# Keys, values and queries as a first Strassen group, the first half's indexer behind it, A11 B11 as first output product

## Chip, cores, metric

The kernel runs on one core of a Trainium2 chip. The metric is device time in microseconds, the median of 3 runs. Engines: PE (TensorE, matrix products into PSUM banks), DVE (VectorE), ACT (ScalarE), POOL (GpSimd), SP (the queue that issues nearly all DMAs). PE waits for the others through semaphores only; every engine works its own instruction list in order.

## What is computed

One layer over 1024 tokens of width 2048, all in float32:

```python
u = einsum('bsd,de->bse', h, w_in)
q, k, v, z_attn, q_idx, k_idx, w_idx, z_ssd, xbc, dt_raw = split_cols(u)
q, k, q_idx, k_idx = partial rotary of each
...
logits = relu(einsum('bqhd,bsd->bqhs', q_idx, k_idx))
score = einsum('bqhs,bqh->bqs', logits, w_idx)      # admissible keys only
_, sel = top_k(score, 256)
o_attn = softmax(q @ k[sel]) @ v[sel] * silu(z_attn)
o_ssd = rmsnorm(ssd(silu(conv(xbc)), dt) * silu(z_ssd))
sub = concat(o_attn, o_ssd) @ w_out
out = layer_norm(2 ** 0.25 * h + sub)
```

The two large products are the input projection (2048 to 6752 columns) and the output projection (2048 to 2048). Eight query heads of 128, two key/value heads, 16 indexer heads of 64, 16 SSD heads in 4 groups.

## The kernel before

**Precision and tiles.** Each float32 operand is split in a high part, rounded to the matmul's short float (ACT copies: `wh`, `xh`), and a low part, the rest (DVE or POOL subtracts: `wl`, `xl`). A product is three matmuls: high x high, high x low, low x high. The tokens are two halves of 512 (h = 0, 1; queries of half 1 may look at all keys). The projection's columns are tiles of 128: `q` 8, `k` 2, `v` 2, `z` 8 (attention gate), `qi` 8 (indexer), `misc` (indexer key, its weights, dt), `xbc` 16 and `zs` 8 (SSD and its gate).

**Stages.** The work on PE is a list of *pieces*, made in `units` (L591): a piece is one tile of 128 columns times 8 of the 16 k-blocks times 512 tokens, 24 matmuls into a PSUM bank `pj`. A plain tile is two pieces. `STAGES` (L56) lists the plain ones: (half 0: misc and the first xbc), (half 1: misc, 8 qi, the 12 k/v/q tiles, 4 xbc), (half 0: k/v, qi at half width, q). `GROUPS` (L61) then lists 14 pairs of tiles (6 of xbc, 8 of z with zs) that are computed with Strassen's scheme, in Winograd's form: with a pair of tiles, the two token halves and the two k-halves as 2x2 blocks, 7 products of 24 matmuls each instead of 8 pieces. The seven products run in four phases over all pairs (2, 2, 2, 1 products); `product` (L661) sets their weights, which are sums of blocks made by DVE from two or three loads (`t_wacc`, L871), one of them (T3) stored and loaded back; partial results P1, U2, U3 go to memory and come back (`t_save`, `t_u3`, `pre_ld`, `t_ld`), and `t_comb` (L735) adds them on DVE. The other operand is one of seven *sets* of 8 tiles each: blocks of x or their sums, which `t_xform` (L779) makes and stores once. `request` loads a set when an older one is done, `t_xst` (L762) splits it. Two sets fit.

**Output projection.** One Strassen-Winograd scheme over the whole matrix: `PRODUCTS` (L68) gives the order of the seven products. Their left operands are made from the layer's mixed outputs in memory, `mx0` and `mx1` (eight attention heads, then eight SSD blocks, per half): `t_form` (L1003) loads and adds, `t_st` splits. A11 is the attention part of half 1, A21 that of half 0, S3 = A11 - A21. The weight sums T1 to T4 are made in the background by `t_wsum` (L810) and kept in memory (`ts`).

**Background.** Indexer scores (`t_qi`, L1446, and `t_score`), the search for each query's 256th score (`t_topk`, L1511, mostly ACT passes), attention (`t_kv`, `t_attn`), the SSD scan (`t_ssd`), gates. These are generator tasks with priorities.

**What sets the order.** At build time a planner (`Flow`, with a cost model of the engines in `Sim`) emits the pieces in list order and lets tasks step in between when their priority, buffers (28 of 256 KB in pool `u`, 8 of 512 KB in `s4`) and expected times allow. Hooks start things at a piece's number: the input sums at piece 40, the output sums at 12 with priority 6. The list that results is fixed; the chip runs it with semaphores.

Of the kernel before, what the change touches and what calls it, by code (L numbers as in the profile page):

```python
# [15 lines left out]
D = 2048  # L16
# [25 lines left out]
def tile_order():  # L42
# [13 lines left out]
STAGES = [  # L56
    (0, FIRST + [("xbc", (0, 2)), ("xbc", (0, 3))], 2),
    (1, [("misc", 0)] + QI + KVQ + [("xbc", (0, j)) for j in range(4)], 3),
    (0, KVQ[:4] + QI + KVQ[4:], 3),
]  # L60
# [7 lines left out]
PRODUCTS = (("S3", "T3"), ("A11", "B11"), ("S1", "T1"), ("S2", "T2"), ("A22", "T4"), ("S4", "B22"), ("A12", "B21"))  # L68
# [501 lines left out]
class Layer:  # L570
# [20 lines left out]
    def units(self):  # L591
# [19 lines left out]

        for h, tiles, end in STAGES:
            n = len(self.sets)
            self.sets += [("x", h, 0), ("x", h, 1)]
            for part in [tiles[:3]] + [[t] for t in tiles[3:-end]] + [tiles[-end:]]:
                for u in range(2):
                    for tile in part:
                        plain(h, tile, u, n)
        for gi, pairs in enumerate(GROUPS):
# [28 lines left out]
        self.hooks.setdefault(40, []).append(self.form_tasks)  # L648
        self.hooks.setdefault(12, []).append(lambda: self.fl.add(self.t_wsum(), 6, "wsum"))
# [160 lines left out]
    def t_wsum(self):  # L810

        fl = self.fl

        def load(name, d, j):
            x = fl.new("s4", [P, 1024])
            fl.dma(x, self.w_block(name, d, j))
            return x
        for d in range(2):
            for j in range(4):
                yield Need("D", s4=4)  # L820
                x, y, z = load("B22", d, j), load("B12", d, j), fl.new("s4", [P, 1024])
                yield Need("V")
                fl.two(z, x, y, ALU.subtract)
                yield Need("")
                fl.dma(self.tsum["T3", d, j], z)
                fl.free(z)
                yield Need("D", s4=1)
# [3 lines left out]
                fl.free(z)  # L831
                yield Need("V")
# [1448 lines left out]
```

## Time and profile before

| | |
|---|---|
| median of 3 runs | 1735.62 us (1734.35 to 1738.17) |
| profiled run | 1736.13 us, of which its span 1734.3 us |
| granted TensorE clock, mean | 0.986 |
| ACT busy | 993.8 us (57%) |
| POOL busy | 176.7 us (10%) |
| memory read / written | 306.32 / 97.65 MB |

A profile names engines by busy time; matmuls overlap, so PE's busy share says when PE had work, and the spacing of matmul starts says what one costs. Windows give, for a stretch of time, each engine's busy time and count, the granted clock, the DMA engines' share and the rate. In a timeline row, brackets hold the idle time before an instruction and what ended it. All operations go through a helper, so one line (L313) stands for all; groups are told apart by names of buffers.

### The profile page before, as it was taken

To read this page: it belongs to the slowest core of one execution; us is meant where nothing else is said; L and a number is where in the kernel's file an instruction comes from. 1 tells how busy PE (TensorE), PEld (TensorE's weight loads), DVE (VectorE), ACT (ScalarE), POOL (GpSimd) and SP (SyncE) were. 2 spreads that over 40 slices of the span, in tenths; PEclk is the share of its full clock that TensorE was granted. 3 is DMA by queue.
4 is the path that set the end of the run, shared out by engine and by line. 5 is a ranking of instruction groups with operands and counts; after the bars stand their busy time and mean duration, and the time that the engine had idled before them with its cause. 6 is when DMAs were issued, how large, how long until landed. Compare 5 with 4: busy or idle time off the path is not lost. (4 is left out here: it accounts for less than half of the span.)

```text
span 1734.3 us, 24108 instructions
## 1 busy us (share of the span) xinstructions
PE 1667.1 (96%) x8188; PEld 1380.5 (80%) x8188; DVE 1293.0 (75%) x2309; ACT 993.8 (57%) x1753; POOL 176.7 (10%) x194
## 2 busy tenths in 40 slices
PE   9999999999999999999999999999999979999987
PEld 7877888787887778888888888777888768888865
DVE  5778866747577778785887678877678757549998
ACT  5755554797797777854555556745775454432320
POOL 0000000000000000121022310302130000000110
PEclk9999999999989999999999999999999989999989
DMA  8543225887643686567863598789979979967654
GB/s 321 191 154 101 84 99 182 280 278 279 208 157 108 205 304 228 195 227 274 309 203 123 182 351 300 252 258 346 314 225 330 327 236 348 343 227 273 213 168 150
DMA packets 185156, 405.58 MB, mean 234 GB/s; under 512 B 19144, under 2 KB 59208, under 8 KB 185032
## 3 DMA queue, kind: packets, MB, share of 16 engines
q1 hardware_dynamic: 184600, 403.65, 68.5%
q8 instruction: 64, 1.05, 0.2%
q14 instruction: 60, 0.49, 0.1%
q10 hardware_dynamic: 432, 0.39, 0.1%
HBM read 306.32 MB, written 97.65 MB: 233 GB/s over the span
## 5 line engine op out<-in xcount | busy, mean ns | idle before, releaser
L313 PE MATMUL pj<-xh,wh 128*128 128x512 f32 (+1 forms) x1264 | 495.9, 392 | 3.4 <-ACT u L313 3.4
L313 PE MATMUL pj<-xh,wl 128*128 128x512 f32 (+1 forms) x1264 | 486.0, 385 | 5.6 <-DVE wl L313 5.6
L313 PE MATMUL pj<-xl,wh 128*128 128x512 f32 (+1 forms) x1264 | 484.9, 384 | 0.0
L313 DVE TENSOR_TENSOR wl<-wr,wh 128x1024 fp32r<-128x1024 f32 (+1 forms) x189 | 230.5, 1220 | 179.8 <-ACT wh L313 176.7
L313 PEld LDWEIGHTS pj<-xh,wl 128*128 128x128 f32 x1264 | 238.3, 189 | 56.1 <-DVE wl L313 8.2
L313 PEld LDWEIGHTS pj<-xh,wh 128*128 128x128 f32 x1264 | 238.7, 189 | 48.3 <-ACT u L313 4.3
L313 PEld LDWEIGHTS pj<-xl,wh 128*128 128x128 f32 x1264 | 238.7, 189 | 42.2 <-DVE xl L313 0.4
L313 ACT ACTIVATE wh<-wr 128x1024 fp32r<-128x1024 f32 (+2 forms) x192 | 198.4, 1034 | 113.8 <-PE pj L313 74.7
L313 PE MATMUL pj<-xh,s 128*128 128x512 f32 (+1 forms) x640 | 204.5, 385 | 2.7 <-ACT wh L313 2.6
L313 PE MATMUL a<-u,u 128*128 128x512 f32 (+3 forms) x766 | 175.8, 352 | 11.2 <-DVE u L313 7.9
L313 PEld LDWEIGHTS a<-u,u 128*128 128x128 f32 x766 | 126.9, 191 | 44.8 <-DVE u L313 12.5
L313 PEld LDWEIGHTS pj<-xh,s 128*128 128x128 f32 x640 | 119.8, 191 | 25.3 <-ACT wh L313 2.8
L313 ACT ACTIVATE u<-u 128x512 f32<-128x512 f32 (+4 forms) x169 | 94.5, 565 | 77.8 <-DVE u L313 64.1
L313 ACT ACTIVATE u<-s,sm 128x768 bf16<-128x768 int16 (+7 forms) x132 | 129.7, 983 | 15.5 <-DVE sm L313 13.5
L313 PE MATMUL pj<-xl,s 128*128 128x512 f32 (+1 forms) x320 | 121.8, 381 | 0.8 <-DVE xl L313 0.8
L313 DVE TENSOR_TENSOR u<-u,u 128x512 f32<-128x512 f32 (+7 forms) x187 | 107.6, 587 | 14.4 <-DMA u<-o 8.3
L313 ACT ACTIVATE a<-a 128x512 f32<-128x512 f32 (+3 forms) x160 | 75.5, 503 | 73.9 <-PE a L313 70.3
L313 ACT ACTIVATE u<-a 128x512 fp32r<-128x512 f32 (+4 forms) x117 | 53.5, 474 | 109.2 <-DVE u L313 56.2
L313 DVE TENSOR_TENSOR wr<-wr,wr 128x1024 f32<-128x1024 f32 (+1 forms) x69 | 88.4, 1283 | 15.3 <-DMA wr<-wt 14.4
L313 ACT ACTIVATE u<-pj 128x512 f32<-128x512 f32 (+1 forms) x83 | 46.1, 561 | 87.7 <-PE pj L313 87.6
L313 PE MATMUL pj<-wh,xh 128*128 128x512 f32 x208 | 84.2, 405 | 8.8 <-DVE xh L313 7.2
L313 DVE TENSOR_TENSOR s<-wr,s 128x1024 fp32r<-128x1024 f32 (+2 forms) x55 | 67.1, 1221 | 31.8 <-ACT s L313 31.8
(262 smaller groups left out, 2633.8 us busy)
## 6 DMA issues: line engine op xcount, KB each, us to landing
wr<-wt SPq DMA_DIRECT2D x222, 512.0 KB, 4.6
s<-wo SPq DMA_DIRECT2D x35, 512.0 KB, 5.4
u<-u SPq DMA_DIRECT2D x70, 256.0 KB, 5.0
ts<-s SPq DMA_DIRECT2D x32, 512.0 KB, 5.6
wr<-ts SPq DMA_DIRECT2D x32, 512.0 KB, 5.4
s<-xt SPq DMA_DIRECT2D x25, 512.0 KB, 9.2
u<-mx SPq DMA_DIRECT2D x42, 256.0 KB, 5.4
wr<-wo SPq DMA_DIRECT2D x20, 512.0 KB
```

The costliest lines, as they stand in the source:

```text
L313: f(*args, **kw)
```

## The change

`STAGES` and `GROUPS` become one `PLAN`. Stage two loses the k/v/q tiles; after it stands a first Strassen group of six pairs (k0 k1, v0 v1, q_n q_(n+4)); then the first half's indexer tiles; then the old group with z and zs exchanged within their pairs. The first output product is A11 B11, S3 T3 the second. The input sums start at piece 12. The output sums are made in halves of 512 columns in buffers of `u`, with two hooks and priority 5. Attention keeps fewer buffers, and both head groups of half 0 wait for half 1's second only.

```diff
+PLAN = [
     (0, FIRST + [("xbc", (0, 2)), ("xbc", (0, 3))], 2),
-    (1, [("misc", 0)] + QI + KVQ + [("xbc", (0, j)) for j in range(4)], 3),
-    (0, KVQ[:4] + QI + KVQ[4:], 3),
-]
-GROUPS = [
-    [(("xbc", (1, j)), ("xbc", (3, j))) for j in range(4)] + [(("xbc", (2, j)), ("xbc", (2, 2 + j))) for j in range(2)]
-    + [(("z", n), ("zs", (n // 2, n % 2))) for n in range(8)],
+    (1, [("misc", 0)] + QI + [("xbc", (0, j)) for j in range(4)], 3),
+    [(("k", 0), ("k", 1)), (("v", 0), ("v", 1))] + [(("q", n), ("q", n + 4)) for n in range(4)],
+    (0, QI, 3),
+    [(("xbc", (1, j)), ("xbc", (3, j))) for j in range(4)] + [(("xbc", (2, j)), ("xbc", (2, 2 + j))) for j in range(2)]
+    + [(("zs", (n // 2, n % 2)), ("z", n)) for n in range(8)],
 ]
+GROUPS = [x for x in PLAN if isinstance(x, list)]
...
-PRODUCTS = (("S3", "T3"), ("A11", "B11"), ("S1", "T1"), ("S2", "T2"), ("A22", "T4"), ("S4", "B22"), ("A12", "B21"))
+PRODUCTS = (("A11", "B11"), ("S3", "T3"), ("S1", "T1"), ("S2", "T2"), ("A22", "T4"), ("S4", "B22"), ("A12", "B21"))
...
-        self.hooks.setdefault(40, []).append(self.form_tasks)
-        self.hooks.setdefault(12, []).append(lambda: self.fl.add(self.t_wsum(), 6, "wsum"))
+        self.hooks.setdefault(12, []).append(self.form_tasks)
+        for half in range(2):
+            self.hooks.setdefault(12, []).append(lambda half=half: self.fl.add(self.t_wsum(half), 5, "wsum"))
...
     def t_ld(self, name, gi, c, ph, f, e):
-        yield Need("", u=1, ev=(self.ev_save[name, gi, c],))
+        yield Need("", u=1, keep=2, ev=(self.ev_save[name, gi, c],))
...
-    def t_wsum(self):
+    def t_wsum(self, half):
+        cols = slice(512 * half, 512 * half + 512)
         def load(name, d, j):
-            x = fl.new("s4", [P, 1024])
-            fl.dma(x, self.w_block(name, d, j))
+            x = fl.new("us", [P, 512])
+            fl.dma(x, self.w_block(name, d, j)[:, cols])
...
-                    fl.add(self.t_score(h, i, kh, m, head, b), 2, f"score{h}", fl.t)
+                    fl.add(self.t_score(h, i, kh, m, head, b), 0.5, f"score{h}", fl.t)
...
-            yield Need(ev=(self.ev_att(*ATT[at - 1]),))
+            yield Need(ev=(self.ev_att(*ATT[min(at - 1, 1)]),))
...
         for (x, hh), (hi, lo) in out.items():
-            yield Need(u=1)
-            raw = fl.new("u", [P, HALF])
-            fl.dma(raw, self.k_sc[hh][g * P:g * P + P] if x == "k" else self.v_sc[hh][g])
+            fl.dma(f32(lo), self.k_sc[hh][g * P:g * P + P] if x == "k" else self.v_sc[hh][g])
+        for hi, lo in out.values():
             yield Need("A")
-            fl.act(hi, raw)
-            yield Need("G")
-            fl.two(lo, raw, f32(hi), ALU.subtract)
-            fl.free(raw)
+            fl.act(hi, f32(lo))
+            fl.two(lo, f32(lo), f32(hi), ALU.subtract)
```

How the built order moves. On PE, half 0's first key tile before: one bank takes 16 k-blocks; here the last rows of its first eight (weights 3793) and the first rows of the next tile, in its own bank and with the same tiles of x from the start (xh, xl are parts of x; wh, wl of the weights).

```order
L313 MATMUL pj_3850<-xl_3705,wh_3793 128x512
L313 MATMUL pj_3850<-xh_3704,wl_3794 128x512
L313 MATMUL pj_3900<-xh_3639,wh_3846 128x512
L313 MATMUL pj_3900<-xl_3640,wh_3846 128x512
L313 MATMUL pj_3900<-xh_3639,wl_3847 128x512
```

On PE after, the new group's start: the first product of pairs one and two (banks 2668 and 2720), then the second product of pair one into the same bank with another set of x.

```order
L313 MATMUL pj_2720<-xh_2483,wh_2595 128x512
L313 MATMUL pj_2720<-xl_2484,wh_2595 128x512
L313 MATMUL pj_2720<-xh_2483,wl_2596 128x512
L313 MATMUL pj_2668<-xh_2611,wh_2664 128x512
L313 MATMUL pj_2668<-xl_2612,wh_2664 128x512
L313 MATMUL pj_2668<-xh_2611,wl_2665 128x512
```

The set of x now changes within a bank's products, and a product serves more than one output. On DVE after, in the same place: `wr` rows are the new weight sums, `wl` splits, `s` with `wsc` the last indexer scores of half 1, the `u` row an output sum.

```order
L313 SCALAR_TENSOR_TENSOR s_216_1240<-a_2990,wsc_244,s_216_1240 128x512
L313 TENSOR_TENSOR wl_3010<-wr_2641,wh_3009 128x1024
L313 TENSOR_TENSOR wr_2958<-wr_2958,wr_2959 128x1024
L313 SCALAR_TENSOR_TENSOR s_216_1240<-a_3020,wsc_244,s_216_1240 128x512
L313 SCALAR_TENSOR_TENSOR s_213_1237<-a_3032,wsc_244,s_213_1237 128x512
L313 SCALAR_TENSOR_TENSOR s_213_1237<-a_3044,wsc_244,s_213_1237 128x128
L313 TENSOR_TENSOR u_3000<-u_2956,u_3000 128x512
L313 TENSOR_TENSOR wl_3077<-wr_2831,wh_3076 128x1024
L313 TENSOR_TENSOR wr_2831<-wr_2831,wr_2958 128x1024
L313 TENSOR_TENSOR wr_3053<-wr_3053,wr_3054 128x1024
```

Between two splits (two pieces of PE work) DVE now has three weight sums beside scores. On SP before, in the first output product: loads of S3's operands (a pair `mx1`, `mx0` for each k-block), stores of `mx1` between them.

```order
L313 DMA u_2418_13317<-mx1_4_275 128x512
L313 DMA xl_2419_13319<-mx0_4_259 128x512
L313 DMA xh_2424_13336<-mx1_5_276 128x512
L313 DMA u_2425_13338<-mx0_5_260 128x512
L313 DMA mx1_6_277<-u_2386_13147 128x512
L313 DMA u_2428_13365<-mx1_0_271 128x512
```

On SP after, in the group's last phase: A11's operands, one load for each k-block.

```order
L313 DMA u_2472_13190<-mx1_2_273 128x512
L313 DMA u_2476_13204<-mx1_3_274 128x512
L313 DMA u_2477_13212<-mx1_4_275 128x512
L313 DMA mx0_4_259<-u_2459_13139 128x512
L313 DMA u_2478_13221<-mx1_5_276 128x512
L313 DMA u_2479_13223<-mx1_6_277 128x512
```

The first product's loads stand ahead of it, and the stores of `mx1` that they read some places earlier.

More of the change, by code (lines that the diff above doesn't have):

```diff
@@ L610, in plain @@
             put(p)
[L612 to L619, printed above, removed]
+        for pairs in PLAN:
+            if isinstance(pairs, tuple):
+                h, tiles, end = pairs
+                n = len(self.sets)
+                self.sets += [("x", h, 0), ("x", h, 1)]
+                for part in [tiles[:3]] + [[t] for t in tiles[3:-end]] + [tiles[-end:]]:
+                    for u in range(2):
+                        for tile in part:
+                            plain(h, tile, u, n)
+                continue
+            gi = GROUPS.index(pairs)
             a11 = len(self.sets)
@@ L808, in t_xform, with save @@
         fl.signal(self.ev_xf[kp])
-    def t_wsum(self):
+    def t_wsum(self, half):
         fl = self.fl
+        cols = slice(512 * half, 512 * half + 512)
         def load(name, d, j):
-            x = fl.new("s4", [P, 1024])
-            fl.dma(x, self.w_block(name, d, j))
-            return x
+            x = fl.new("us", [P, 512])
+            fl.dma(x, self.w_block(name, d, j)[:, cols])
+            return x
+        def save(name, d, j, x):
+            fl.dma(self.tsum[name, d, j][:, cols], x)
         for d in range(2):
             for j in range(4):
-                yield Need("D", s4=4)
-                x, y, z = load("B22", d, j), load("B12", d, j), fl.new("s4", [P, 1024])
+                yield Need("D", u=2, keep=6)
+                x, y = load("B22", d, j), load("B12", d, j)
                 yield Need("V")
[L823 to L827, printed above, removed]
+                fl.two(x, x, y, ALU.subtract)
+                yield Need("D", us=1)
+                save("T3", d, j, x)
+                fl.free(x)
                 z = load("B11", d, j)
@@ L842, in t_wsum @@
                 yield Need("")
-                fl.dma(self.tsum["T4", d, j], z)
+                save("T4", d, j, z)
                 fl.free(z)
-                fl.signal(self.ev_wsum[4 * d + j])
+                fl.signal(self.ev_wsum[half][4 * d + j])
     def w_src(self, src):
@@ L933, in w_summed @@
         p = self.stream[i]
-        return p.kind != "O" or p.load[0][1][0] != "T" or self.ev_wsum[4 * p.t + p.u].t is not None
+        return p.kind != "O" or p.load[0][1][0] != "T" or all(e[4 * p.t + p.u].t is not None for e in self.ev_wsum)
     def w_can(self, i):
@@ L1302, in start_tasks @@
         self.tsum = {(f"T{n}", d, j): self.scratch(f"ts{n}_{d}{j}", [P, 1024]) for n in (1, 2, 3, 4) for d in range(2) for j in range(4)}
-        self.ev_wsum = [Event() for _ in range(8)]
+        self.ev_wsum = [[Event() for _ in range(8)] for _ in range(2)]
         self.s2_sc = [self.scratch(f"s2_{kk}", [P, HALF]) for kk in range(8)]
@@ L1730, in load @@
                 fl.signal(self.ev_mask[i])
-            rg = fl.new("us", [P, 2, P])
-            fl.dma(rg, src(self.q_sc, pr, i * P - h * HALF))
-            return i, pr, rg
+            qq = fl.new("us", [P, 2, 2, P], R)
+            fl.dma(f32(qq[:, 1]), src(self.q_sc, pr, i * P - h * HALF))
+            return i, pr, qq
         loaded = None
@@ L1742, in t_attn @@
                 loaded = load()
-            i, pr, rg = loaded
+            i, pr, qq = loaded
             loaded = None
@@ L1747, in t_attn @@
             heads = (2 * pr, 2 * pr + 1)
-            yield Need("A", ev=(self.ev_mask[i],), us=1, s4=1 + h)
+            yield Need("A", ev=(self.ev_mask[i],), s4=1 + h)
             kv = st["kv"]
-            raw = rg
-            qq = fl.new("us", [P, 2, 2, P], R)
             qh, ql = qq[:, 0], qq[:, 1]
@@ L1757, in t_attn @@
                 pt = [fl.new("s4", [P, 1024]) for _ in heads]
-            fl.act(qh, raw)
+            fl.act(qh, f32(ql))
             yield Need("G")
-            fl.two(ql, raw, f32(qh), ALU.subtract)
-            fl.free(rg)
+            fl.two(ql, f32(ql), f32(qh), ALU.subtract)
             yield Need("", sm=1)
@@ L1844, in t_attn_out @@
                 fl.spare_u = 2
[L1845 removed]
+        if h == 0:
+            self.nout += 1
+            if self.nout == 16:
                 fl.free(self.mask[2])
```

15 lines of the change are left out of this document (8 added, 7 removed).

## Prediction

> **What bounds the kernel now.** I read the page's head first, then the windows by stage, then the chain of waits, then the groups by form.
>
> ```profile
> span 1734.3 us, 24108 instructions
> ...
> PE 1667.1 (96%) x8188; PEld 1380.5 (80%) x8188; DVE 1293.0 (75%) x2309; ACT 993.8 (57%) x1753; POOL 176.7 (10%) x194
> ...
> DMA packets 185156, 405.58 MB, mean 234 GB/s; under 512 B 19144, under 2 KB 59208, under 8 KB 185032
> ```
>
> TensorE (PE) is busy 96% of the span, VectorE (DVE) 75%. What one matmul costs is read from the chain of waits, where PE runs without a stop, and, for half-wide ones, from the timeline:
>
> ```profile
> 1513.75 47.60 PE pj L313 x210
> ```
> ```profile
> 479.78 0.28 PE L313 MATMUL pj<-xh,wh 128*128 128x256 f32 x1
> 479.90 0.28 PE L313 MATMUL pj<-xl,wh 128*128 128x256 f32 x1
> ```
>
> 47.60 us for 210 is 0.2267 us for a 512-wide matmul; the half-wide ones start 0.12 us apart. The groups by form name a longer time for the same instruction:
>
> ```profile
> L313 PE MATMUL pj<-xh,wl 128*128 128x512 f32 x1176 | 460.5, 392 | 5.0 <-DVE wl L313 5.0
> ...
> L313 DVE TENSOR_TENSOR wl<-wr,wh 128x1024 fp32r<-128x1024 f32 x183 | 227.5, 1244 | 174.2 <-ACT wh L313 171.1 <-PE a L313 2.4 <-DMA s<-xt 0.3
> ...
> L313 DVE TENSOR_TENSOR wr<-wr,wr 128x1024 f32<-128x1024 f32 x68 | 87.2, 1284 | 15.3 <-DMA wr<-wt 14.4
> ...
> L313 DVE TENSOR_TENSOR u<-pj,u 128x512 f32<-128x512 f32 x54 | 37.1, 688 | 23.2 <-PE pj L313 18.7 <-DMA u<-p 2.7 <-DMA z<-u 1.5
> ...
> L313 DVE TENSOR_TENSOR xl<-xr,xh 128x512 fp32r<-128x512 f32 x55 | 35.6, 694 | 8.4 <-ACT xh L313 8.3
> ...
> L313 ACT ACTIVATE xh<-xr 128x512 fp32r<-128x512 f32 x55 | 31.6, 621 | 18.7 <-DMA xr<-xt 10.4 <-DMA xr<-xfM 7.2 <-DMA xr<-xfS 0.6
> ```
>
> 392 ns is the length of one, with its neighbours inside it. A removed matmul is worth its spacing. (The Trainium skill, Trace Analysis, "Identifying the Most-Contended Engine", says that matmul busy time is a poor measure because matmuls are pipelined; the trace agrees, 392 ns long at 227 ns apart. By busy time 144 matmuls would be an estimated 56 us.)
>
> The stages, cut where the count of projection matmuls reaches a stage's end (64.6: end of the first; 409.3: end of the second half's 25 tiles; 622.4: the group begins, its four phases end at 836.1, 1050.7, 1265.2, 1369.4; then the output products):
>
> ```profile
> core 0: us, PE busy (x) PEld busy (x) DVE busy (x) ACT busy (x) POOL busy (x), PEclk, DMA share, GB/s
> ...
> 64.60:409.30 344.70, 339.48 (x1547) 274.95 (x1546) 246.61 (x445) 213.58 (x381) 11.21 (x16) 1.00 0.52 176
> 409.30:622.40 213.10, 204.33 (x1077) 173.92 (x1076) 157.82 (x352) 171.58 (x308) 4.68 (x5) 0.98 0.57 187
> 622.40:836.10 213.70, 208.29 (x1060) 175.44 (x1059) 160.85 (x326) 137.47 (x284) 25.62 (x21) 0.99 0.72 252
> ...
> 1050.70:1265.20 214.50, 205.58 (x1062) 170.50 (x1061) 168.84 (x302) 133.70 (x245) 40.40 (x50) 0.99 0.87 290
> ...
> 1369.40:1442.50 73.10, 60.63 (x317) 49.25 (x316) 47.01 (x82) 36.50 (x69) 2.45 (x3) 0.91 0.84 278
> 1442.50:1491.40 48.90, 48.90 (x241) 40.46 (x240) 35.53 (x53) 18.86 (x31) 2.29 (x2) 1.00 1.03 366
> ```
>
> PE bounds every stage but one. In the stretch 64.6 to 836.1, which the change rewrites, DVE is busy 246.61 + 157.82 + 160.85 = 565 of 771.5 us (73%) and the DMA rate is 176 to 252 GB/s: there is room on both. The exception is the first output product (1369.4 to 1442.5): 73.1 us, clock 0.91.
>
> **The change, part by part.** *1. The twelve key, value and query tiles as six Strassen pairs.* Before, 12 tiles x 2 halves x 16 k-blocks x 3 = 1152 matmuls of 512 columns; after, 6 pairs x 7 products x 8 x 3 = 1008. **144 x 0.2267 = -32.6 us**, all on PE, which bounds the stage; in the order the count of PE's matmuls falls by exactly 144.
>
> The pairs are paid for on other engines. Per pair five additions of weight blocks, five combining additions on results; and seven sets of the input, 8 tiles each, are loaded and split: DVE 30 x 1.284 + 30 x 0.688 + 56 x 0.694 = 98 us, less six splits of weights (42 against 48, x 1.244 = 7.5): **+90 us of DVE**. ScalarE (ACT): 56 x 0.621 = 35 us more, less the same six splits; it is 57% busy and is covered. The new waits are those of the combining additions for partial results that come back from memory; behind one on DVE stand splits of weights and inputs, for which PE waits. The u<-pj,u row has 2.7 us of such waits in 54: 1.5 us for 30 more, within the bounds below. Counted on SP's queue in the order, 87.6 MB are issued inside the new group: 11 weight transfers of 0.52 MB and 7 of 0.26 MB a pair (46 MB), seven sets of 2.1 MB (15 MB), the rest the output sums and what stood there anyhow.
>
> Does PE cover this? Of background work, about 36 us of PE's and as much of DVE's (attention, gates) is moved in the order out of the stretch into the group's later phases, where the 1265.2 row still has DVE at 79% (168.84 of 214.5). The stretch would then be 771.5 - 32.6 - 36 = 703 us of PE, with 565 + 90 - 36 = 619 us of DVE in it: 88%. The nearest rows at such a share are those in which the second half's indexer runs:
>
> ```profile
> 100.00:150.00 50.00, 47.17 (x213) 37.37 (x212) 42.97 (x76) 28.45 (x57) 0.00 (x0) 1.00 0.33 112
> 150.00:200.00 50.00, 49.87 (x235) 39.58 (x234) 43.16 (x69) 26.98 (x49) 0.88 (x2) 1.00 0.33 100
> ...
> 1150.00:1200.00 50.00, 45.77 (x238) 37.47 (x237) 34.62 (x58) 25.54 (x44) 10.13 (x6) 0.97 0.97 337
> ...
> 1450.00:1500.00 50.00, 49.09 (x238) 40.22 (x237) 36.53 (x53) 19.99 (x30) 2.29 (x2) 1.00 1.03 378
> ```
>
> DVE at 86% leaves PE 97.0 of 100 us: 3% lost, where the stretch as it was lost 19.4 of 771.5 (2.5%). And DMA: the group's 1008 matmuls are 228.5 us, its few other PE rows some 17 us: 87.6 MB in 246 us is 356 GB/s. Rows at that load stand above: 378 GB/s at share 1.03 with PE at 98%, 337 GB/s at 0.97 with PE at 92%. So the bounds of what the group costs PE by late weights and sets are 0 (the 1450 row held) and +50 us: that is 87.6 MB plus the 18.2 MB of the first half's indexer behind it at 290 GB/s (the 1050.7 row) = 365 us, against 246 + 50 (384 half-wide matmuls x 0.12, and 4) of PE work, less the 20 us that the old stages there already lost. I take **+10**, nearer the low end, since the group now in the kernel passes its phase boundaries (836.1, 1050.7) at clocks of 0.99 and more, with the same sets of the input changing there and DMA at 0.7 to 0.9.
>
> (The Trainium skill, DMA: Bandwidth & Descriptors, "Specifications", puts the memory's limit at about 358 GB/s for a core. This speaks against the change: an estimated 245 us for the 87.6 MB, as long as PE's own 246, so every late issue would be lost time. The 1450 row's 378 GB/s lies above it, so the trace does not show that limit as a hard one over 50 us.)
>
> *2. The first half's indexer after the group, first half's masks later.* The same instructions; the mask that first-half attention needs is ready during the long group, and the first half's attention outputs, stored in the third and last phases before, are stored in the last after (one in the first product). **0**; the cover is the long group's some 700 us. If it failed, first-half attention would land in the second product: part of rival B.
>
> *3. A11 B11 first.* What stands in the first product's idle time now:
>
> ```profile
> 1394.87 0.80 PE L313 MATMUL pj<-xr,xh 128*128 128x512 f32 x1 [2.50 <-ACT xh L313]
> ...
> 1404.25 0.79 PE L313 MATMUL pj<-xr,xh 128*128 128x512 f32 x1 [7.73 <-ACT xh L313]
> ```
> ```profile
> 1393.46 0.69 DVE L313 TENSOR_TENSOR xh<-xh,xl 128x512 f32<-128x512 f32 x1 [3.12 <-DMA xl<-mx]
> ```
>
> S3 is A11 - A21, so each tile waits for two loads of mixed outputs, some stored a few queue places earlier. A11 needs one load, of second-half heads long stored; S3's are made while A11 runs. The product's 192 matmuls are 43.5 us, its 125 small ones, at the next row's (48.9 - 43.5) / 49 = 0.11 us each, 13.8: the hole is 73.1 - 57.3 = **16 us**. At most 16 goes, at least none (what is late next is S3 itself, or DMA, at 366 GB/s in the next product). I take **-10**.
>
> *4. Output sums in halves, started with priority 5.* 32 subtractions of 1024 become 64 of 512 (+3 us of DVE) and 8 blocks of 0.5 MB are read twice (+4 MB). In the order the last sum is stored in the long group's second phase, before in the first product: out of the full place. What of it falls into the new group is in the 87.6 MB. *5. Attention loads its raw tile straight into the low part; scores at priority 0.5; both first-half attentions may run together.* The same arithmetic, fewer buffers held: **0** by itself, bounds -5 and +5 (the 3% of the 100:200 rows, either way). The pairs z and zs change places: the same work, 0.
>
> **Sum**, against the profiled run's own 1736.13 us (its span is 1734.3, so 1.8 lie around it; the median of the runs shown is 1735.62, half a microsecond less): -32.6 + 10 - 10 + 0 = -32.6, **1704 us** to the nearest.
>
> **The rivals.**
>
> *A, cleaner than that.* The group costs nothing and the hole goes whole: 1736.1 - 32.6 - 16 = 1687, down to 1680 if the 8.8 us that PE stood idle between 409.3 and 622.4 go with the old stage. For it: the 1450 row. Against it: DVE at 88% over 700 us has no row.
>
> *B, the group is bound by DVE or DMA, or the hole only moves to S3.* The 105.8 MB at 310 to 300 GB/s are 341 to 353 us, +25 to +37, with the hole unrecovered: 1736.1 - 32.6 + 25 = 1728; 1722 to 1740. For it: 337 GB/s with PE at 92%.
>
> *C, slower.* One mechanism: at each phase boundary of the short group both sets change within 16 us of PE time, eight loads of 0.5 MB behind weights on the one SP queue; with a phase of 65 us instead of 152 the queue never gets ahead, and the group runs at the DMA rate. It decides from 292 GB/s down: the 105.8 MB of group and indexer then take 362 us, against 296 of PE and the 20 that the old stages lost, +46 where the sum has +10. At 283 GB/s they take 374: 1704 + 48 = **1752**. For it: 278 GB/s in the first product and 290 in the third phase. Against it: neither of those was at a full DMA share (0.84, 0.87).
>
> *D, the change doesn't do what it says*: A11 first, but its tiles late too. The order has the second half's eight head outputs stored before the last phase's end; only the 10 us of part 3 hang on it: 1714, inside the forecast's own range.
>
> **How the numbers follow.** Forecast 1704 (1690 to 1721): 0.55. A: 0.15. B: 0.17, of which 0.10 ends faster by over 0.2%, 0.05 within, 0.02 slower. C: 0.13, of which 0.01 within 0.2%. 0.2% is 3.5 us, about what a measurement of this kernel can tell from no change. Faster 0.80, same 0.06, slower 0.14. The range runs from A's low end to the +50 of the 290 GB/s bound, 1680 to 1745; it leaves out some 0.04 below and 0.11 above.
>
> **What would show it.** 144 fewer 512-wide pj matmuls at 0.2267 us; the group's windows at 250 to 270 us with DVE near 90% and DMA near 0.95; the first product at 50 to 60 us and clock near 1.0. Wrong if PE in the group waits over 40 us for wl, xh or xl behind DMA, or if the second product takes the hole over.

## The result and the profile after

The changed kernel takes 1728.33 us (median of 7 runs, 1722.52 to 1731.08) where the kernel before, in the same batch, takes 1740.09 (7 runs): ratio 0.9937, 95% interval 0.9918 to 0.9956. It is 11 to 12 us faster, where the prediction had 32.6; the forecast was 1704 (1690 to 1721). The profiled run took 1725.14 us, span 1723.4; a second measurement (c0_same) gave 0.9929 (0.9907 to 0.9950).

The head of the page of after:

```profile
span 1723.4 us, 24378 instructions
...
PE 1638.7 (95%) x8044; PEld 1351.2 (78%) x8044; DVE 1353.0 (79%) x2444; ACT 1019.6 (59%) x1799; POOL 173.5 (10%) x201
...
DMA packets 210215, 446.50 MB, mean 259 GB/s; under 512 B 21928, under 2 KB 61992, under 8 KB 210088
```

TensorE issues 8044 matmuls, 144 fewer, as in the order; DVE works 60 us more in the whole kernel, and 41 MB more are moved. The groups of after by form show where the extra work went:

```profile
L313 DVE TENSOR_TENSOR wl<-wr,wh 128x1024 fp32r<-128x1024 f32 x173 | 210.9, 1221 | 108.0 <-ACT wh L313 107.3
L313 DVE TENSOR_TENSOR wr<-wr,wr 128x1024 f32<-128x1024 f32 x96 | 119.2, 1243 | 20.5 <-DMA wr<-wt 19.4
...
L313 DVE TENSOR_TENSOR u<-pj,u 128x512 f32<-128x512 f32 x84 | 57.7, 687 | 36.3 <-PE pj L313 31.0 <-DMA u<-u 4.3 <-DMA mx<-u 0.8
L313 DVE TENSOR_TENSOR xl<-xr,xh 128x512 fp32r<-128x512 f32 x89 | 56.9, 686 | 23.9 <-ACT xh L313 23.8
```

The counts bear the prediction's out (30, 30, 56 and 6): 28 more weight sums (two more run on POOL), 30 more combining additions, 34 more splits of input tiles in `xr` (19 more read buffers of `s`), 10 fewer weight splits in this form.

The windows of after by stage, cut as before by the count of projection matmuls: second stage 63.8 to 258.9; the new group to 546.6 (its third and fourth phases begin at 412.1 and 508.3), the first half's indexer to 615.7; first phase of the long group to 806.2; output products from 1359.6. Columns as in the windows of before.

```profile
core 0: us, PE busy (x) PEld busy (x) DVE busy (x) ACT busy (x) POOL busy (x), PEclk, DMA share, GB/s
63.80:258.90 195.10, 189.25 (x845) 152.69 (x844) 169.28 (x260) 112.50 (x197) 11.72 (x12) 0.99 0.65 228
258.90:615.70 356.80, 317.71 (x1581) 263.07 (x1580) 278.25 (x546) 246.14 (x436) 14.50 (x15) 0.96 0.82 284
615.70:806.20 190.50, 183.27 (x847) 148.74 (x846) 161.05 (x352) 144.92 (x298) 5.02 (x7) 1.00 0.85 290
```
```profile
412.10:508.30 96.20, 77.47 (x331) 59.63 (x329) 58.12 (x139) 67.30 (x123) 2.48 (x2) 0.93 0.79 272
508.30:546.60 38.30, 36.49 (x152) 29.20 (x153) 29.08 (x59) 25.91 (x49) 0.00 (x0) 0.94 0.86 295
546.60:615.70 69.10, 54.87 (x425) 52.89 (x424) 59.36 (x119) 52.46 (x87) 2.81 (x2) 0.93 0.68 239
...
1359.60:1419.30 59.70, 58.48 (x309) 47.39 (x308) 40.46 (x76) 30.89 (x62) 9.88 (x7) 1.00 0.97 306
1419.30:1477.90 58.60, 56.10 (x306) 45.96 (x305) 41.44 (x72) 28.55 (x59) 0.00 (x0) 1.00 1.01 350
```

Two things stand out. The first output product is 13 us shorter, at full clock. And the group with the indexer behind it takes 356.8 us at clock 0.96, where the prediction counted some 296 us of TensorE work (228.5 + 17 + 50). Of the 61 us lost there TensorE is idle for 356.8 - 317.7 = 39; the other 22 are matmuls that took longer than was counted for them. Stage by stage, the stretch up to the long group's second phase is 771.5 - 742.4 = 29.1 us shorter, the long group's other three phases 20.1 longer (553.4 against 533.3, with 132 more matmuls: background work that came to stand there), the products and what follows 1.1 shorter (with 136 more), the first stage 0.8.

Where TensorE stands in the group is read from its timeline of after (in brackets: idle time, and what ended it):

```profile
430.97 0.79 PE L313 MATMUL pj<-xh,wh 128*128 128x512 f32 x1 [3.52 <-ACT xh L313]
...
437.45 0.69 PE L313 MATMUL pj<-xh,wh 128*128 128x512 f32 x1 [3.26 <-ACT xh L313]
...
461.46 0.80 PE L313 MATMUL pj<-xh,wl 128*128 128x512 f32 x1 [3.55 <-DVE wl L313]
...
508.30 0.80 PE L313 MATMUL pj<-xh,wh 128*128 128x512 f32 x1 [5.79 <-ACT wh L313]
...
558.74 0.58 PE L313 MATMUL pj<-xh,wh 128*128 128x256 f32 x1 [9.09 <-ACT wh L313]
```

The waits for weights and input tiles in the group and the indexer (us in total, times, longest) are 30 of the 39 us:

```profile
PE pj L313 <- ACT wh L313: 16.4, 3, 9.1
PE pj L313 <- DVE wl L313: 6.9, 7, 3.6
PE pj L313 <- ACT xh L313: 6.8, 2, 3.5
```

The longest, 9.09 us at the indexer's start, can be followed back through SP's timeline, what SP waited for from 538 to 544, and then ACT's timeline:

```profile
538.46 4.97 SPq L313 DMA_DIRECT2D xr<-xt  x2
...
545.10 1.04 SPq L313 DMA_DIRECT2D s<-xt  x2
```
```profile
SPq L313 <- DMA k<-u: 4.1, 1, 4.1
```
```profile
549.02 2.42 ACT L313 ACTIVATE xh<-xr 128x512 fp32r<-128x512 f32 x4 [4.44 <-DMA xr<-xt]
555.34 2.41 ACT L313 ACTIVATE xh<-s 128x512 fp32r<-128x512 f32 x4 [3.89 <-DMA s<-xt]
557.65 1.99 ACT L313 ACTIVATE wh<-wr 128x1024 fp32r<-128x1024 f32 x2
```

The indexer's input set is issued from 538.5 on; between its first two loads SP stood 4.1 us until an earlier store (`k`) had landed. Its later tiles, issued at 545, land only when ACT's wait ends at 555.3. Behind them in ACT's list stands the weight split that TensorE waits for. ACT is idle meanwhile, and the transfers are in a lull, as the busy tenths of the DMA engines and the rates of the indexer's stage (546.6 to 615.7, 40 slices of 1.73 us) show from the fourth slice on:

```profile
DMA  9972342228689899998720064903444999999989
GB/s 281 346 299 104 140 168 109 98 99 268 168 327 404 250 403 320 408 285 273 225 90 0 0 242 168 277 24 116 192 152 138 408 396 405 415 408 306 275 247 308
```

So these tiles are late by their place in SP's list and by some 10 us under way. Up to the lull, in the first slices of the stage, the DMA engines are busy for 70 to 90% of the time; in the last 3.5 us before the landing it is 20 to 40%, so full engines are not the whole reason. What holds the tiles in the lull no run shows.

### The profile page after: what moved, and what is told of

The parts are those of the page before. It is cut to its first block, busy times and chain, and to the rows that moved or that the text cites. A ratio compares the mean times of both kernels' runs of the same rounds, so it can differ in the third digit from the quotient of the medians.

```text
span 1723.4 us, 24378 instructions
## 1 busy us (share of the span) xinstructions
PE 1638.7 (95%) x8044; PEld 1351.2 (78%) x8044; DVE 1353.0 (79%) x2444; ACT 1019.6 (59%) x1799; POOL 173.5 (10%) x201
## 5 line engine op out<-in xcount | busy, mean ns | idle before, releaser
L313 PE MATMUL pj<-xh,wh 128*128 128x512 f32 (+1 forms) x1192 | 470.0, 394 | 25.9 <-ACT wh L313 18.0
L313 PE MATMUL pj<-xh,wl 128*128 128x512 f32 (+1 forms) x1192 | 460.1, 386 | 9.3 <-DVE wl L313 9.1
L313 PE MATMUL pj<-xl,wh 128*128 128x512 f32 (+1 forms) x1192 | 458.8, 385 | 0.1
L313 DVE TENSOR_TENSOR wl<-wr,wh 128x1024 fp32r<-128x1024 f32 (+1 forms) x179 | 213.9, 1197 | 113.2 <-ACT wh L313 112.6
L313 ACT ACTIVATE wh<-wr 128x1024 fp32r<-128x1024 f32 (+1 forms) x185 | 190.6, 1033 | 106.7 <-PE pj L313 67.2
L313 PE MATMUL pj<-xh,s 128*128 128x512 f32 (+1 forms) x688 | 222.1, 385 | 1.8 <-DVE u L313 1.6
L313 DVE TENSOR_TENSOR u<-u,u 128x512 f32<-128x512 f32 (+7 forms) x212 | 130.2, 627 | 16.1 <-DMA u<-wo 4.5
L313 ACT ACTIVATE u<-s,sm 128x768 bf16<-128x768 f32 (+7 forms) x132 | 129.6, 982 | 21.3 <-DVE sm L313 19.5
L313 DVE TENSOR_TENSOR wr<-wr,wr 128x1024 f32<-128x1024 f32 (+1 forms) x98 | 121.6, 1243 | 20.5 <-DMA wr<-wt 19.4
L313 ACT ACTIVATE u<-u 128x512 f32<-128x512 f32 (+4 forms) x165 | 91.9, 566 | 61.5 <-DVE u L313 57.3
L313 DVE TENSOR_TENSOR u<-pj,u 128x512 f32<-128x512 f32 (+2 forms) x94 | 62.4, 664 | 36.7 <-PE pj L313 31.0
```

The source lines that it names most:

```text
L313: f(*args, **kw)
```

## The experiments

In the table, "front" is the time from the end of the first stage to the start of the long group (64.6 to 622.4 before), "long" the long group, P1 to P3 the first three output products, all from one profiled run each. Ratios are to the kernel before, measured in the same batch. Six kernels (e6, e7, e10, e11, p1, p2) lie above every range that was written down for them.

| kernel | ratio (95%) | front | long | P1 | P2 | P3 |
|---|---|---|---|---|---|---|
| before | 1 | 557.8 | 747.0 | 73.1 | 48.9 | 46.6 |
| after | 0.9937 (0.9918-0.9956) | 551.9 | 743.9 | 59.7 | 58.6 | 53.6 |
| c0_same | 0.9929 (0.9907-0.9950) | 552.2 | 749.5 | 59.7 | 59.0 | 53.6 |
| e1_plain | 0.9971 (0.9949-0.9992) | 589.6 | 734.5 | 57.1 | 48.5 | 45.4 |
| e2_s3first | 0.9956 (0.9936-0.9976) | 549.9 | 742.8 | 61.1 | 57.7 | 59.1 |
| e3_a11only | 1.0017 (1.0002-1.0032) | 556.8 | 755.3 | 53.8 | 74.0 | 46.0 |
| e4_sums_late | 1.0047 (1.0024-1.0070) | 546.9 | 748.0 | 58.0 | 59.0 | 79.4 |
| e5_plan_5us | 1.0177 (1.0143-1.0212) | 572.8 | 740.9 | 57.6 | 70.6 | 72.7 |
| e6_qi_first | 1.0088 (1.0071-1.0105) | 547.4 | 738.9 | 67.2 | 52.1 | 85.4 |
| e7_no_subtraction | 1.0021 (0.9998-1.0045) | 565.6 | 748.1 | 57.3 | 56.5 | 51.0 |
| e9_sums | 1.0001 (0.9984-1.0018) | 570.9 | 756.6 | 69.5 | 47.7 | 43.5 |
| e10_attention | 1.0119 (1.0096-1.0143) | 575.5 | 754.4 | 70.0 | 51.1 | 44.6 |
| e11_group | 1.0146 (1.0130-1.0162) | 547.2 | 735.8 | 133.3 | 44.9 | 43.5 |
| t1_dve_less | 0.9866 (0.9845-0.9888) | 543.9 | 744.3 | 58.5 | 58.5 | 54.2 |
| t2_dma_less | 0.9766 (0.9743-0.9788) | 527.0 | 740.7 | 59.4 | 60.6 | 53.6 |
| t3_sums_pool | 0.9968 (0.9951-0.9984) | 555.4 | 746.6 | 59.3 | 60.7 | 53.6 |
| t4_topk_less | 0.9878 (0.9856-0.9899) | 548.1 | 744.2 | 58.2 | 59.4 | 53.6 |
| t6_all_less | 0.9725 (0.9704-0.9746) | 525.0 | 739.6 | 57.7 | 58.5 | 53.6 |
| p1_split_pool | 1.0088 (1.0068-1.0108) | 581.3 | 746.7 | 57.7 | 59.5 | 53.6 |
| p2_low_pool | 1.0036 (1.0020-1.0052) | 569.6 | 746.8 | 58.6 | 62.0 | 53.6 |

### The group back out, and three changes that the planner sees

e1_plain keeps the rest of the change and makes the twelve tiles plain again:

```diff
-    (1, [("misc", 0)] + QI + [("xbc", (0, j)) for j in range(4)], 3),
-    [(("k", 0), ("k", 1)), (("v", 0), ("v", 1))] + [(("q", n), ("q", n + 4)) for n in range(4)],
-    (0, QI, 3),
+    (1, [("misc", 0)] + QI + KVQ + [("xbc", (0, j)) for j in range(4)], 3),
+    (0, KVQ[:4] + QI + KVQ[4:], 3),
```

> The changed kernel with the six pairs as plain tiles again (the key, value and query tiles back in the two stages of before); all other parts of the change kept. By the matmul count it would be 32.6 us slower than the changed kernel, 1757 to 1761. Theory L (in the short group and the indexer behind it loads land late, and the in-order queues of ACT, DVE and SP pass the delay on to PE) and theory V (DVE at 85% is the bound there) both say the group gives most of its 32.6 us back, so that this kernel is only 3 to 12 us slower than the changed one: 1730 to 1740. If it is as fast as the changed one or faster, the whole gain comes from A11 first and the smaller parts.

Measured: 1735.25 us, 0.9971. Against it the change gains 0.3 to 0.4%, some 6 us of 32.6 on paper, and the rest of the change is worth some 5; the intervals of the two ratios just overlap, and e1_plain too has a list of its own, so the 6 us hold the group and the new list together. e4_sums_late starts the output sums at piece 94 instead of 12, e7_no_subtraction leaves the 64 subtractions of those sums out, and e5_plan_5us lets the planner expect each load 5 us after its issue instead of 2.5:

```diff
-            self.hooks.setdefault(12, []).append(lambda half=half: self.fl.add(self.t_wsum(half), 5, "wsum"))
+            self.hooks.setdefault(94, []).append(lambda half=half: self.fl.add(self.t_wsum(half), 5, "wsum"))
...
-                fl.two(x, x, y, ALU.subtract)
...
-    LAND = 2500.0
+    LAND = 5000.0
```

> The output sums start at piece 94, with the long group, and not at piece 12: none of their loads, stores and subtractions lie in the short group. Theory W (the sums' DMA traffic is what makes the group's loads late) and theory V (their DVE time is what is too much) say 10 to 20 us faster, 1708 to 1718. If loads are late for the group's own traffic and the order of the queues, at most 5 us faster, or slower where the sums then fall on the first products.

> The output sums' loads and stores stay, their 64 subtractions are left out (the output products use unsubtracted blocks). 44 us of DVE go, half of it in the short group and the indexer behind it. Theory V: 10 to 20 us faster, 1708 to 1718. Theory L or W: within 4 us of the changed kernel, as DMA is the same.

> The planner counts on 5.0 us instead of 2.5 us from the end of a transfer to its landing; nothing else. Weight loads landed in 9.5 us (median) in the last phases of the short group. Theory L: the order then asks earlier or puts other work in front of what waits, 5 to 15 us faster, 1713 to 1723, with fewer waits of PE for ACT's splits. Theory V: no change or slower, as DVE's work is the same.

All three came out slower than the change, by 1.1, 0.9 and 2.4% (from 0.9933, the mean of the change's two measurements). Late sums shorten the front by 5 us but open a hole in the third product (79.4 us); fewer subtractions made the front 14 us longer. That can't be the price of work left out: the planner sees each of these edits and writes another list for the whole kernel. Such variants compare lists, not only costs. The next ones keep the list.

### The same list with smaller instructions

t1, t2, t4 and t6 tell the planner the full instruction and emit a smaller one in its place, so every engine's list of instructions is that of the change.

```diff
+    def two_part(self, out, a, b, op):
+        eng = self.pick(out.free_size(), a, b)
+        c = slice(0, 128)
+        (self.nc.vector if eng == "V" else self.nc.gpsimd).engine.tensor_tensor(out=out[:, c], in0=a[:, c], in1=b[:, c], op=op)
+        self.placed(self.sim.run(eng, "tensor_tensor", [out], [a, b], {}))
...
-        fl.two(x, x, parts[1], p.op)
+        two(x, x, parts[1], p.op)
```

> The change, with every instruction in the change's own order; only the sizes of some VectorE instructions are cut: the 30 sums and differences of weights of group 1 and the 64 subtractions that make the output product's weight sums work on 128 columns instead of 1024 or 512 (so the outputs are not the reference's). About 30 x (1.23 - 0.2) + 64 x (0.65 - 0.2) = 60 us less VectorE work, nearly all of it inside the second stage and group 1; the transfers are the same. Theory V (group 1 is bound by VectorE, 79% of the span and up to 87% in its phases): 10 to 25 us faster than the change, ratio 0.980 to 0.988 to the kernel before. Theory L (the losses come from transfers that land late, and the queues of ScalarE, VectorE and SyncE pass the delay on in order): within 5 us of the change, 0.991 to 0.997.

t2 adds the same for transfers:

```diff
+    def dma_as(self, out, in_, o, i):
+        self.nc.sync.engine.dma_start(o, i)
+        self.placed(self.sim.run("SP", "dma_start", [out], [in_], {}))
...
-            for x, src in zip(parts, p.load):
-                fl.dma(x, self.w_src(src))
+            for k, (x, src) in enumerate(zip(parts, p.load)):
+                y, c = self.w_src(src), 128 if k and p.kind == "T" and p.key[0] == 0 else 1024
+                fl.dma_as(x, y, x[:, :c], y[:, :c])
```

> As t1_dve_less, in the same order, and with fewer bytes: the 18 blocks that group 1 adds to another block are loaded in 128 of 1024 columns, and the weight sums of the output product are loaded and saved in 128 of 512 columns (later loads of those sums take a weight block in their place). Some 18 x 0.46 MB and 54 x 0.2 MB, 19 of the 84 MB that pass between 259 and 546 us, are gone. Theory L: the waits behind late transfers in group 1 shrink by a third to a half of the 61 us lost there, 10 to 30 us faster than t1_dve_less. Theory V or a bound in ScalarE's order (T): within 5 us of t1_dve_less.

> The change in its own order; the counting passes of the second half's top-k on ScalarE work on 64 columns instead of up to 1024 (so its masks are not the reference's). Theory T (ScalarE meets the weights and inputs of group 1 behind counting passes, which are themselves released by VectorE one by one): 5 to 15 us faster than the change, 0.985 to 0.991. Theory L: within 4 us of the change, 0.991 to 0.996.

```diff
-                    fl.act(junk[:, 0:(i + 1) * P], src, AF.Sign, bias=bias[:, j:j + 1], accum_out=count[:, j:j + 1])
+                    if h == 0:
+                        fl.act(junk[:, 0:(i + 1) * P], src, AF.Sign, bias=bias[:, j:j + 1], accum_out=count[:, j:j + 1])
+                    else:
+                        fl.nc.scalar.engine.activation(junk[:, 0:64], src[:, 0:64], AF.Sign, bias=bias[:, j:j + 1], accum_out=count[:, j:j + 1])
+                        fl.placed(fl.sim.run("A", "activation", [junk[:, 0:(i + 1) * P], count[:, j:j + 1]], [src, bias[:, j:j + 1]], dict(func=AF.Sign)))
```

> The change's own order with all three cuts at once: less VectorE work (t1_dve_less), fewer bytes (t2_dma_less) and short counting passes (t4_topk_less). If the three engines hand the same delays on (one cut helps where another would have helped too), it lies within 4 us of t2_dma_less, 0.974 to 0.979. If each has delays of its own, the gains add up: 8 to 10 us below t2_dma_less, 0.970 to 0.973. In the profile group 1 and the indexer behind it then take 320 to 335 us, against some 296 us of TensorE work; what is left is order and latency, not the load of any one engine.

> The change itself once more, as the measure for the kernels of this batch and the last. Every theory: ratio 0.994 to the kernel before, within 0.002, as in the first measurement; the stages as in the first profile within 3 us each.

The windows from the second stage's end to the long group's start: t1_dve_less, t2_dma_less, t4_topk_less, and all three cuts together:

```profile
258.10:607.80 349.70, 318.54 (x1582) 266.25 (x1581) 242.21 (x545) 246.46 (x437) 9.00 (x15) 0.95 0.83 289
```
```profile
258.10:591.10 333.00, 312.85 (x1581) 263.62 (x1580) 242.00 (x545) 245.66 (x436) 8.38 (x15) 0.97 0.73 246
```
```profile
260.10:612.90 352.80, 317.40 (x1582) 264.19 (x1581) 278.46 (x547) 183.47 (x436) 16.68 (x15) 0.96 0.83 287
```
```profile
258.60:589.30 330.70, 312.13 (x1581) 264.36 (x1580) 243.75 (x545) 183.36 (x436) 9.32 (x15) 0.96 0.74 247
```

Against 356.8 and 355.6 us in the two profiles of the change, 36 us less DVE work takes 6 to 7 off, the smaller transfers another 17, 63 us less ACT work 3 to 4; all together 25 to 26. By medians the ratio falls by 0.0067 (t1), by a further 0.0100 (t2 behind t1: 17 us), by 0.0055 (t4), and by 0.0208 for all: 36 us, close to the sum of the three, 0.0222. The transfers count most, and no single engine is the bound: V, L and T each got the gain that it expected of its own cut, and each had expected nothing of the others'. Of T's 10 us by medians, though, only 3 to 4 lie in this stretch. c0_same met its ratio, not all its stages: the long group took 749.5 us there, 5.6 more, so single stages of single profiles carry an error of that size.

Some 35 us over 296 are left in t6_all_less. TensorE is idle for 330.7 - 312.1 = 18.6 of them, 15.8 in three places of its timeline; the other 16 are matmuls that took longer than was counted, for which the clock of 0.96 gives an estimated 0.04 x 330.7 = 13:

```profile
425.76 0.80 PE L313 MATMUL pj<-xh,wh 128*128 128x512 f32 x1 [4.78 <-ACT xh L313]
...
489.00 0.80 PE L313 MATMUL pj<-xh,wh 128*128 128x512 f32 x1 [4.90 <-ACT wh L313]
...
534.85 0.58 PE L313 MATMUL pj<-xh,wh 128*128 128x256 f32 x1 [6.07 <-ACT wh L313]
```

In this run the third phase begins at 405.7, the fourth at 489.0, the indexer at 525.8. The three waits end 20 us after the first of these changes of sets, at the second, and 9 us after the third. They outlast a cut of 19% in bytes (101 to 82 MB in that window, rate by time).

### Other queues

> The change in its own order; the 144 transfers of the output product's weight sums are issued from POOL's queue instead of SP's, nothing else. Theory S (SP's queue, which issues everything in order, stands at a transfer that waits for VectorE, and the loads of group 1 behind it start late): 5 to 15 us faster than the change, 0.985 to 0.991. Theory L without S (the engines of the DMA are what is late, whoever issues): within 4 us, 0.991 to 0.996. Slower than 1.0 if POOL's own work, x1 of the masks, stands ahead of the transfers.

```diff
+    def dma_pool(self, out, in_):
+        self.nc.gpsimd.engine.dma_start(out, in_)
+        self.placed(self.sim.run("SP", "dma_start", [out], [in_], {}))
...
-            fl.dma(x, self.w_block(name, d, j)[:, cols])
+            fl.dma_pool(x, self.w_block(name, d, j)[:, cols])
```

Measured: 1734.99 us, 0.9968, somewhat slower than the change, with a front of 555.4 us. Fewer issues on SP's queue did not shorten the group; theory S falls.

p1_split_pool and p2_low_pool take the splits of late input tiles out of the lists of ACT and DVE:

```diff
+    def split_pool(self, hi, lo, raw, both):
+        if both:
+            self.nc.gpsimd.engine.tensor_scalar(out=hi, in0=raw, scalar1=1.0, scalar2=1.0, op0=ALU.mult, op1=ALU.mult)
+        else:
+            self.nc.scalar.engine.activation(hi, raw, AF.Copy)
...
+        self.nc.gpsimd.engine.tensor_tensor(out=lo, in0=raw, in1=f32(hi), op=ALU.subtract)
...
+            if 5 <= n <= 12:
+                fl.split_pool(hi, lo, raw[:, e], True)
```

> The change in its own order; the input tiles of group 1's later six sets and of the indexer behind it (64 tiles) get both halves of their split on POOL instead of ScalarE and VectorE: some 64 x (0.73 + 1.29) = 129 us on POOL, which is busy 15 of 357 us there; the same result. If late input tiles hold up weight splits behind them in the in-order queues of ScalarE and VectorE (31 us of waits of ScalarE for such tiles in the stretch): 6 to 15 us faster than the change, ratio 0.984 to 0.990. If bytes alone are late, or POOL's slower splits make the sets late in their turn: within 4 us of the change or slower, 0.991 to 1.003.

> As p1_split_pool, but only the low half of the split goes to POOL; the high half stays on ScalarE in its place. If ScalarE's queue is where weight splits stand behind late tiles: no better than half of what p1_split_pool gains, 0.989 to 0.994. If it is VectorE's load (44 us less of it): as p1_split_pool or better.

Measured: 1752.10 us (1.0088) and 1744.12 us (1.0036): both slower than the change. The waits in the group and the indexer (us in total, times, longest), first of c0_same, then of p1_split_pool (up to 640, 6 us before its indexer ends):

```profile
PE pj L313 <- ACT wh L313: 14.2, 2, 8.6
PE pj L313 <- DVE wl L313: 7.1, 7, 3.5
PE pj L313 <- ACT xh L313: 6.6, 2, 3.4
```
```profile
PE pj L313 <- POOL xl L480: 12.5, 16, 1.7
PE a L313 <- DMA u<-c: 10.9, 1, 10.9
...
PE pj L313 <- POOL xh L475: 4.6, 5, 1.2
PE pj L313 <- DVE wl L313: 4.2, 3, 2.7
PE pj L313 <- ACT wh L313: 2.3, 1, 2.3
```

The weights are on time once no input tile stands ahead of them: 14.2 us of waits for `wh` become 2.3. In p2_low_pool, where the high halves stay in ACT's list, they are 14.7. So the chain read above, late tile, then weight split in ACT's list, is real. But the input tiles themselves are then late, 17 us of waits for POOL's slower splits, and a buffer that is split later is loaded later (SP stood 22.0 us at one load behind a POOL split). The sets have no lead to give away: in these two kernels the splits are on the path wherever they are done.

### The first product

e2_s3first puts S3 T3 back in front in the changed kernel; e3_a11only puts A11 B11 in front in the kernel before:

```diff
-PRODUCTS = (("S3", "T3"), ("A11", "B11"), ...
+PRODUCTS = (("A11", "B11"), ("S3", "T3"), ...
```

> The change with the old order of the output products, S3 T3 ahead of A11 B11; the planner's order in the last stages changes with it. If the hole in the first product is worth the 10 to 16 us that I gave it: first product 70 us or more again, and 8 to 16 us slower than the change, 0.999 to 1.003. If the later sums and the first half's later masks had already filled that hole: within 4 us of the change.

> The kernel before with nothing but the new order of the output products, A11 B11 first. If the hole is worth 10 to 16 us by itself: first product 57 to 62 us, clock near 1.0, ratio 0.991 to 0.994. If S3, now second, is late in its turn: second product 60 us or more and 0.997 to 1.0.

With S3 first the change keeps a first product of 61.1 us, in which TensorE is busy throughout, and loses 0.3% at most. A11 first alone shortens the first product to 53.8 us and lengthens the second to 74.0; the kernel is 0.17% slower. In e3_a11only TensorE's idle time in that second product is ended by these two:

```profile
1486.63 1.83 PE L313 MATMUL a<-o,xl 128*128 128x1 f32 x8 [10.56 <-DVE xl L313]
...
1494.06 0.79 PE L313 MATMUL pj<-wh,xh 128*128 128x512 f32 x1 [5.59 <-ACT wh L313]
```

The first is background work, the second waits for a weight, not for a tile of S3: the hole has passed to other waits. Further kernels ask which other part filled it: e9_sums has only the sums in halves (new `t_wsum` and its hooks, first diff), e10_attention only the edits to `t_kv`, `t_attn`, `t_score` and `t_ld` (second, cut); e11_group has only the new plan, with input sums at piece 12; e6_qi_first swaps two lines of the plan (third).

```diff
-        self.hooks.setdefault(12, []).append(lambda: self.fl.add(self.t_wsum(), 6, "wsum"))
+        for half in range(2):
+            self.hooks.setdefault(12, []).append(lambda half=half: self.fl.add(self.t_wsum(half), 5, "wsum"))
```
```diff
-                    fl.add(self.t_score(h, i, kh, m, head, b), 2, f"score{h}", fl.t)
+                    fl.add(self.t_score(h, i, kh, m, head, b), 0.5, f"score{h}", fl.t)
...
-            yield Need(ev=(self.ev_att(*ATT[at - 1]),))
+            yield Need(ev=(self.ev_att(*ATT[min(at - 1, 1)]),))
```
```diff
     (1, [("misc", 0)] + QI + [("xbc", (0, j)) for j in range(4)], 3),
+    (0, QI, 3),
     [(("k", 0), ("k", 1)), (("v", 0), ("v", 1))] + [(("q", n), ("q", n + 4)) for n in range(4)],
-    (0, QI, 3),
```

> The kernel before with only the output product's weight sums as in the change: in halves of 512 columns, in other buffers, at priority 5. If these sums, the last of which was stored within the first output product, were what stood in that product's hole: first product 57 to 62 us and ratio 0.990 to 0.995. If not: first product over 68 us and ratio 0.998 to 1.003.

> The kernel before with only the attention's part of the change: raw tiles loaded into the low half, scores at priority 0.5, both first-half attentions at a time, two input tiles kept free by the group's loads. If late attention (its outputs are the mixed outputs that the first product reads) made the hole: first product 57 to 62 us and ratio 0.990 to 0.995. If the sums made it: first product over 68 us and 0.998 to 1.003.

> The kernel before with only the group of six pairs and the first half's indexer behind it (and the swapped pairs of the long group): sums, attention and product order are those of before. If the group alone nets about what e1 says, 4 to 10 us: ratio 0.994 to 0.998, with the hole of the first product still there. If it needs the smaller buffers of the other parts to run at all well: 1.0 to 1.01.

> The change with the first half's indexer ahead of the group instead of behind it. The indexer's 16 weight pieces then come before the group's load, and the group runs straight into the long group, two boundaries in a row. If the order in which engines meet their work in the group decides, 0.990 to 1.000, either side of the change; if the bytes decide, the same bytes in the same stretch: within 4 us of the change, 0.991 to 0.996.

Neither part alone fills the hole: first products of 69.5 and 70.0 us. With both, without the group (e1_plain, with A11 first) it is 57.1, and with both and the group but S3 first (e2) 61.1. A kernel with both alone, S3 first and no group, was not run, so that these two together fill the hole is argued and not shown. The group alone is 24 us slower than before, though it is ahead until the products begin: its first product takes 133.3 us.

```profile
1348.40:1481.70 133.30, 103.78 (x552) 84.35 (x551) 85.11 (x181) 64.48 (x149) 18.87 (x26) 0.86 0.75 257
```

It holds 552 matmuls, where that of after has 309: background that did not run earlier has piled up there. In e11_group front and long group together are 22 us shorter than before (1283.0 against 1304.8), two thirds of the group's 32.6, and 60 come back in one product. e6_qi_first, the indexer ahead, has the same front as the change within 5 us (547.4) and its hole in the third product, 85.4 us.

## Why the prediction was wrong in size

- **144 fewer matmuls, -32.6:** right. The count fell by 144, and one still costs 0.2267 us where TensorE runs on.
- **The group's price, +10:** this is the term that was mis-sized. By the prediction's own measure (296 us of work, and the 20 us that the old stages had lost too) the group and the indexer came to 356.8 - 296 - 20 = **+41**; over the whole stretch, 742.4 - (771.5 - 32.6 - 36) = +39.5. It chose the low end of 0 to +50 because the long group passes its phase boundaries at clocks of 0.99 and more with the same sets. That was the wrong row: the long group has 28 pieces a phase, 152 us; the new one has 12, 65 us, and its waits stand at its changes of sets. What the runs showed in place of +10 is a loss of 61 us, of which smaller DVE work, transfers and ACT passes take back 26 (17 of them the transfers) and 35 stay. That the short phase is the reason is read from where the waits stand; no run varied the length of a phase.
- **How the sum closes:** in the spans of the two profiles the stretch gained 29.1 us where the prediction had 32.6 + 36 - 10 = 58.6. The moved background cost 20.1 us in the long group's later phases where its sum implies 36, products and what follows gained 1.1 where it had 10, and the first stage 0.8: 10.9 us in all, not 32.6. So 29.5 us were lost on the group and 9 on the products, and 16 of them came back because the background cost less than was counted. That last gain was not forecast.
- **DVE near 90%:** it was 278.25 of 356.8 us, 78%, and 58.12 of 96.2 (60%) in the phase with the most idle time of TensorE. A full DVE was not the reason; yet t1 shows that less DVE work still helps, by 6 to 7 us; that splits stand in DVE's list behind other work is the likely way, not a shown one.
- **DMA near 0.95:** the mean was 0.82, 284 GB/s. The rate was what rival C priced (105.8 MB at 283 GB/s, 374 us; here 101 MB passed in 356.8), and t2 shows that bytes count: fewer of them, 17 us. But a mean rate is not the whole limit: at 246 GB/s t2 still takes 333 us.
- **The hole, -10 by A11 first:** the hole went (73.1 to 59.7 us), and A11 first is not what closed it: with S3 first (e2) it is closed too. A11 first is worth -0.2 to 0.3% in its two trials. The other parts, which the prediction put at 0, matter there; the sums in halves and the attention's buffers together are the likely ones. Second and third product are 10 and 7 us longer, with 65 and 80 more matmuls, at full clock: much of what was won is only moved.
- **"Wrong if PE in the group waits over 40 us for wl, xh or xl":** this sign did not come, and the term was wrong all the same. The waits there for weights and tiles are 30 us; with a clock of 0.96 and other waits the loss is 61. The threshold was set on one part of the loss.
- **The rivals:** B gave the time measured, 1728, for another reason (a group at +25 with the hole unrecovered); that agreement is luck. C's mechanism is the nearest to what the runs show, waits at the changes of sets and a gain from fewer bytes, at +41 where C's 1752 has 10 + 48 = +58; but the group does not simply run at the DMA rate, since the engines' share was 0.82 and 35 us stay when 19% of the bytes are gone.

What stays open is how much of the 35 us left in t6_all_less is latency of single transfers and how much their order in SP's list; a list with the same work and the sets issued earlier was not tried. Which part closed the hole stays open too. Of the kernels that do all of the work none is faster than the change.

## What to carry to other kernels

Price a new stage by the length of its phases too, and not by its mean load alone: at a change of inputs the next ones need a lead, and here, with phases of 65 us, they had none at several changes, with DVE at 78% and the DMA engines at 82%. Work saved on a bounding engine is kept only if the background finds room elsewhere: follow it to the end of the program (e11_group won 22 us and lost 60). Where a planner writes the order, compare costs with the order held fixed; edits that it sees moved the time by up to 2.4%, whatever they were about.

## What the runs showed of the hardware

**Landing times under a bursty load.** The issues of the window 412:508 of after, and of the window 412:622 of before (KB each, median us to landing):

```profile
wr<-wt SPq DMA_DIRECT2D x17, 512.0 KB, 9.5
```
```profile
wr<-wt SPq DMA_DIRECT2D x42, 512.0 KB, 3.3
```

The same transfer takes three times as long at a mean of 272 GB/s as at 189; the first window's 40 slices swing between 72 and 422 GB/s. The rate alone doesn't set it: the indexer's tiles above took 10 us and landed in a lull. (The prediction's aside went by 358 GB/s for a core. The Trainium skill, Perfetto Trace Analysis, "Roofline", says that this is the share with two active cores and that a single one can pull more, bounded at about 435; the 422 GB/s of a slice here, above 358 and under 435, agree with that.)

**The clock after a wait.** TensorE's timeline of after, behind the 9.09 us of idle time at 558.74:

```profile
560.38 0.42 PE L313 MATMUL pj<-xh,wh 128*128 128x256 f32 x1
560.60 0.41 PE L313 MATMUL pj<-xl,wh 128*128 128x256 f32 x1
...
563.80 0.32 PE L313 MATMUL pj<-xl,wh 128*128 128x256 f32 x1
563.96 0.28 PE L313 MATMUL pj<-xh,wl 128*128 128x256 f32 x1
564.07 0.28 PE L313 MATMUL pj<-xh,wh 128*128 128x256 f32 x1
```

Half-wide matmuls start 0.21 us apart from 560.38 to 563.80 and 0.12 us apart from 563.96 on. A wait thus costs more than its length; here 16 distances at 0.1 us each, some 1.5 us, in these rows alone. (The Trainium skill, TensorE: Matmul & The Clock Gate, "Part 1: The HAM clock gate", has the clock halved after an idle window of about 3.4 us and restored after as long a busy one; the trace agrees in kind, with 5.2 us here from the first matmul behind the wait, at 558.74, to full rate, and one more wait of 0.46 us among the first three.)

**Issuing from POOL.** In t3_sums_pool a transfer costs POOL's list about 0.55 us:

```profile
L478 POOL DMA_DIRECT2D u<-wo x79 | 43.6, 554 | 98.4 <-DVE sm L313 81.6 <-DVE s L313 9.2 <-DMA wr<-wt 5.9
```
